# Down projections as seven products of half-size blocks, in three pieces a layer, and the attention bias kept as one row a head

## The chip, the cores and the metric

The kernel runs on one core of a Trainium2 chip, as one launch. The metric is the device time of that launch in microseconds. Below, PE is the matrix engine (its weight loads are listed apart, as PEld), DVE the vector engine, ACT the scalar engine, POOL the general-purpose engine and SP the engine that issues most DMAs. Each engine works through its own queue strictly in order; an instruction that needs another engine's result waits at the head of its queue, and all that is queued behind it waits too.

## What is computed

A trunk of two decoder layers over 512 tokens of width 1024, in float32. Layer 0 mixes tokens by a gated DeltaNet, layer 1 by sliding-window attention with a relative-position bias. Each layer ends with a gated MLP of inner width 2816, and that is where the change lies:

```python
def conv_gated_mlp(hn, w_up, conv_w, conv_b, w_down):
    u = causal_dwconv(hn @ w_up, conv_w, conv_b)
    gate, val = jnp.split(u, 2, axis=-1)
    return (jax.nn.silu(gate) * val) @ w_down

# in the trunk, for each of the two layers
h = h + conv_gated_mlp(rmsnorm(h, ffn_norm_w[layer]), ...)

# in the attention: one bias value for each head and distance between query and key
bias = rel_table[t5_bucket(dist)]
s = einsum(q, k) + bias, masked to 0 <= dist < 128
```

## The kernel before

Activations lie transposed: 128 features on the partitions, 512 tokens along the free axis. The residual `h` is eight such tiles, two neighbours of which lie in one buffer. Every float32 operand of a large product is kept as two reduced-precision parts, `hi` (a rounded copy) and `lo` (what is left), and a product is three matmuls (`mm3`, L132 to L137): hi by hi, hi by lo and lo by hi.

Weights come in stages: `load_stage` (L116) has SP load up to eight 128x256 tiles into one of two `stage` buffers. `cast` (L124) makes the two parts of one 128-wide half of a stage: ACT copies to `whi` (L128), then DVE subtracts to `wlo` (L129). There are three `whi` and three `wlo` buffers, so a cast waits until PE has finished with the cast three back.

The gated MLP (`ffn`, L830) splits the 22 tiles of the inner width into two pieces, of 12 and 10 tiles. In a piece it first makes the activations, two tiles (a pair) at a time. For a tile, `up` (L839) runs 24 matmuls of 512 columns for the gate and 24 for the value. Each result is scaled (DVE, L843), put through the width-3 convolution (ACT L846, then two DVE instructions at L848), the gate through a Silu (ACT, L863), and both are multiplied (DVE, L865). `split` then writes the two parts (ACT L140, DVE L141) into buffers handed out in turn by `wide`; there are 16 of these. When the whole piece is there, each of the eight output tiles `m` is summed over all its tiles, as 12x3 or 10x3 matmuls of 512 columns into one PSUM bank of tag `d`, and DVE adds the bank to `h[m]` (L881).

The last output tile of layer 1 goes through `final` (L891), which runs its matmuls in two halves of 256 tokens, so that the closing norm of the first half runs beside the second; two running sums feed it (DVE L898 and L904). After layer 0, `attention` normalises `h` (ACT L144, DVE L145), adds up its squares (L796) and starts with the K and V projections, whose weights are cast by the same L128 and L129.

The attention bias is made once, by `bias_rows` (L680): PE picks the table's rows by a one-hot product, DVE writes a row of 257 values a head, and POOL issues four DMAs (L691) that write that row 128 times into the scratch tensor `rb`. Later each pair of heads reads a 128x2x256 block of it (L995), and DVE adds it to the scores (L1018).

The order within each queue is set at build time by a list scheduler: it places instructions by priority (program order here) as its own estimate says that they become ready, so the order may differ from the program's, but it is fixed when the kernel runs.

## Time and profile before

| | |
|---|---|
| three timed runs | 1463.84 to 1468.73 us, median 1468.68 us |
| the profiled execution | 1466.23 us, of which the recorded span is 1464.3 us |
| TensorE clock granted, mean | 0.992 |
| PE, DVE, ACT, POOL busy share | 98%, 65%, 49%, 2% |
| down projections, one piece of 12 tiles | about 66 us (8 output tiles of 8.24 us) |

A row of the profile names the line of the code, the engine, the operation and its operands as output<-inputs; a timeline row begins with the start in us from the span's start and the duration. Matmuls overlap in the array, so the time that one adds is the distance between two starts, not its recorded duration. The release named behind an idle time is the instruction that ended the wait.

### The profile page before, as it was taken

What the parts mean: (1) busy time and instruction counts of PE and PEld (TensorE: products, weight loads), DVE (VectorE), ACT (ScalarE), POOL (GpSimd) and SP (SyncE); (2) the same over time, 40 slices, a digit from 0 to 9 for tenths busy, and PEclk for the clock granted to TensorE, in tenths of its full rate; (3) what the DMA queues carried; (4) which work ended last, traced back from release to release, by engine and by line L of the source; (5) the groups of instructions that cost most, each with busy time, mean ns of one, the idle gap of its engine ahead of it and who ended that gap; (6) DMA issues with size and microseconds to landing.
All of it is one profiled execution on the core that took longest, in us unless ns stands there. A gap on an engine that the chain in (4) does not pass through costs nothing.

```text
span 1464.3 us, 19548 instructions
## 1 busy us (share of the span) xinstructions
PE 1438.9 (98%) x7519; PEld 1167.2 (80%) x7519; DVE 951.6 (65%) x1661; ACT 718.3 (49%) x1406; POOL 22.7 (2%) x51
## 2 busy tenths in 40 slices
PE   7999999999999999999999999999999999999998
PEld 5778878878877788878888888877788888888887
DVE  5896885968835536748337765778667775356754
ACT  7764574656536424434224444678744443234432
POOL 1000000000000000000010000000000000000000
PEclk9999999999989999999999999999999999999999
DMA  5334254163346523272332223221132322322222
GB/s 153 97 93 112 84 164 122 55 195 109 109 150 219 167 91 107 70 140 93 108 116 84 89 94 126 91 73 51 46 101 86 115 79 87 121 88 87 94 72 94
DMA packets 163617, 154.79 MB, mean 106 GB/s; under 512 B 24212, under 2 KB 150725, under 8 KB 163525
## 3 DMA queue, kind: packets, MB, share of 16 engines
q1 hardware_dynamic: 160690, 151.25, 32.4%
q0 software_dynamic: 576, 2.11, 1.3%
q8 instruction: 59, 0.97, 0.3%
q10 hardware_dynamic: 2259, 0.20, 0.2%
q14 instruction: 33, 0.27, 0.1%
HBM read 134.65 MB, written 18.88 MB: 105 GB/s over the span
## 4 chain that ended last, share of the span: by engine, by line
PE 93%; DMA 4%; ACT 1%; DVE 1%; issue 0%; ACTq 0%; DVEq 0%; SPq 0%
PE d L137 26%; PE d L135 26%; PE d L136 26%; PE s L585 2%; DMA stage<-in_ffn_w_up_dram 1%; PE p L1043 1%; PE s L600 1%; PE g L1038 1%; PE s L625 1%; PE p L608 1%; PE s L562 1%; PE p L555 1%; PE g L671 1%; PE s L1013 1%; DMA ol<-od 1%; PE g L450 1%
## 5 line engine op out<-in xcount | busy, mean ns | idle before, releaser
L135 PE MATMUL d<-xh,whi 128*128 128x512 f32 x1192 | 475.7, 400 | 2.3 <-ACT whi L128 2.2
L137 PE MATMUL d<-xh,wlo 128*128 128x512 f32 x1192 | 475.3, 400 | 0.1
L136 PE MATMUL d<-xl,whi 128*128 128x512 f32 x1192 | 474.2, 398 | 0.0
L128 ACT CAST whi<-stage 128x1024 fp32r<-128x1024 f32 (+2 forms) x236 | 230.2, 977 | 340.3 <-PE d L136 312.1
L129 DVE TENSOR_TENSOR wlo<-stage,whi 128x1024 fp32r<-128x1024 f32 (+2 forms) x236 | 267.0, 1132 | 151.5 <-ACT whi L128 145.9
L135 PEld LDWEIGHTS d<-xh,whi 128*128 128x128 f32 x1192 | 225.4, 189 | 50.5 <-ACT whi L128 2.6
L136 PEld LDWEIGHTS d<-xl,whi 128*128 128x128 f32 x1192 | 225.3, 189 | 49.2 <-issue 1.2
L137 PEld LDWEIGHTS d<-xh,wlo 128*128 128x128 f32 x1192 | 225.2, 189 | 49.2 <-issue 1.4
L227 DVE SCALAR_TENSOR_TENSOR acc<-d,cwc,acc 128x511 f32<-128x511 f32 (+2 forms) x96 | 70.6, 738 | 8.8 <-ACT acc L224 8.4
L843 DVE TENSOR_TENSOR sz<-d,p6s 128x512 f32<-128x512 f32 x58 | 39.9, 687 | 55.3 <-PE d L137 53.4
L863 ACT ACTIVATE dt<-dt 128x512 f32<-128x512 f32 x44 | 27.8, 632 | 83.3 <-DVE dt L848 83.2
L137 PE MATMUL d<-sy,wlo 128*128 128x512 f32 (+1 forms) x148 | 57.4, 388 | 0.0
L135 PE MATMUL d<-sy,whi 128*128 128x512 f32 (+1 forms) x148 | 57.2, 388 | 0.0
L136 PE MATMUL d<-sy,whi 128*128 128x512 f32 (+1 forms) x148 | 57.2, 386 | 0.0
L135 PE MATMUL d<-kT,whi 128*128 128x512 f32 (+1 forms) x146 | 57.2, 394 | 0.0
L137 PE MATMUL d<-kT,wlo 128*128 128x512 f32 (+1 forms) x146 | 57.1, 391 | 0.0
L136 PE MATMUL d<-qT,whi 128*128 128x512 f32 (+1 forms) x146 | 57.0, 390 | 0.0
L848 DVE SCALAR_TENSOR_TENSOR va<-sz,fcw,va 128x511 f32<-128x511 f32 (+1 forms) x58 | 43.4, 748 | 2.7 <-ACT va L846 1.7
L848 DVE SCALAR_TENSOR_TENSOR dt<-sz,fcw,dt 128x511 f32<-128x511 f32 (+1 forms) x58 | 43.4, 748 | 1.2 <-ACT dt L846 0.2
L507 DVE TENSOR_TENSOR sT<-sT,p6s 64x31 f32<-64x31 f32 (+15 forms) x124 | 40.8, 329 | 1.9
L501 DVE TENSOR_TENSOR p6s<-sN,sT 64x31 f32<-64x31 f32 (+15 forms) x124 | 40.8, 329 | 1.8
L843 DVE TENSOR_TENSOR zl<-d,p6s 128x512 f32<-128x512 f32 x30 | 20.6, 688 | 31.2 <-PE d L137 30.9
(378 smaller groups left out, 2121.7 us busy)
## 6 DMA issues: line engine op xcount, KB each, us to landing
stage<-in_ffn_w_up_dram SPq DMA_DIRECT2D x44, 1024.0 KB, 5.1
stage<-in_a_w_in_dram SPq DMA_DIRECT2D x23, 1024.0 KB, 5.4
stage<-in_ffn_w_down_dram SPq DMA_DIRECT2D x16, 768.0 KB, 4.3
stage<-in_ffn_w_down_dram SPq DMA_DIRECT2D x16, 640.0 KB, 4.1
stage<-in_a_w_out_dram SPq DMA_DIRECT2D x8, 1024.0 KB, 4.8
zd<-sz SPq DMA_DIRECT2D x16, 256.0 KB, 2.0
od<-o SPq DMA_DIRECT2D x16, 256.0 KB, 2.9
stage<-in_b_w_q_dram SPq DMA_DIRECT2D x4, 1024.0 KB, 5.6
```

The costliest lines, as they stand in the source:

```text
L128: S.copy(hi[:, :kt, :m], src)
L129: V.tensor_tensor(lo[:, :kt, :m], src, hi[:, :kt, :m].bitcast(F32), op=ALU.subtract)
L135: PE.matmul(ps, hi[:, k, :m], xh[k], start=first and k == 0, stop=False)
L136: PE.matmul(ps, hi[:, k, :m], xl[k][:], start=False, stop=False)
L137: PE.matmul(ps, lo[:, k, :m], xh[k], start=False, stop=last and k == kt - 1)
L227: V.scalar_tensor_tensor(acc[:, d:], ps[:, : T - d], col, acc[:, d:], op0=ALU.mult, op1=ALU.add)
L501: V.tensor_tensor(tv, N[:, s, s + 1 : 32].unsqueeze(2).to_broadcast([64, n, m]), Tm[:, s : s + 1, 0:m].to_broadcast([64, n, m]), op=ALU.mult,)
L507: V.tensor_tensor(Tm[:, s + 1 : 32, 0:m], Tm[:, s + 1 : 32, 0:m], tv, op=ALU.subtract)
L585: PE.matmul(x[:, si], t[:, i, cs], S0[:, si], start=True, stop=True)
L843: V.tensor_tensor(u[:], ps[:], rs[:], op=ALU.mult)
L848: V.scalar_tensor_tensor(acc[:, d:], u[:, : T - d], tap(2 - d, t), acc[:, d:], op0=ALU.mult, op1=ALU.add)
L863: S.activation(a[:], a[:], AF.Silu)
```

## The change

**Seven products.** Two tiles of the inner width and two output tiles make a 2x2 arrangement of weight blocks (A11, A12, A21, A22, each 128x128), and the two halves of the tokens with the two inner tiles a 2x2 arrangement of activation blocks (B11 to B22, each 128x256). The four output blocks were eight block products; now they are seven, of sums and differences of the blocks (Strassen's scheme in Winograd's form). A block product is three matmuls of 256 columns. For each pair of output tiles and each piece the seven products are summed over the piece's pairs in PSUM banks of the tags d, p, s, g and d (`seven_products`).

For that, the change adds work on three engines:

- DVE, for each pair of activation tiles: four differences of 256 columns (`forms`, L917 to L920), and four `lo` parts in place of two (L930). ACT makes four `hi` copies in place of two (L929).
- POOL, for each pair of output tiles and piece: four sums or differences of weight blocks, in place in the stage (L959, L964, L965, L971), each over 128 x (pairs of the piece) x 128 values.
- ACT and DVE, for each pair of output tiles and piece: three and a half casts of the stage's halves (`cast`, and `cast_odd` for a half one, L137 and L138) in place of two whole ones. DVE adds the products to `h` in six instructions of 256 columns and two of 512, in place of two of 512 (L951).

Each pair of tiles now takes four `wide` buffers, so a piece holds four pairs at most: the 22 tiles go in three pieces, of 8, 8 and 6. The last pair of output tiles of layer 1's last piece is done as before (`plain`).

**Bias.** `rb` is now 16x384, one row a head, written by one DMA from SP; each block is read from it with a window that moves by one value a partition, and DVE reads it backwards along the keys.

```diff
+    def cast_odd(st, nk, half):
...
+        odd = slice(1, 2 * nk, 2)
+        src = st[:, odd, half * P : half * P + P]
+        S.copy(hi[:, odd, :], src)
+        V.tensor_tensor(lo[:, odd, :], src, hi[:, odd, :].bitcast(F32), op=ALU.subtract)
...
-        for u in range(4):
-            G.dma_start(
-                rb[:, 32 * u : 32 * u + 32, :], oh_t[0:16, 144:401].unsqueeze(1).to_broadcast([16, 32, 257])
-            )
...
+        SP.dma_start(rb[:], rv[0:16, 0:384])
...
-        for t0, t1 in ((0, 12), (12, 22)):
+        for t0, t1 in ((0, 8), (8, 16), (16, NF)):
...
-                    split(b[:], gp[:, j, :], lp[:, j, :])
...
+                sevens.append(forms(*f, plain))
...
+                st = load_stage(wdn, t0 * P, 2 * nk, 256 * m2)
+                if not (plain and m2 == KD // 2 - 1):
+                    seven_products(st, nk, sevens, h_pairs[m2])
+                    continue
...
+    def forms(f0, f1, plain):
+        B11, B12, B21, B22 = f0[:, HALF[0]], f0[:, HALF[1]], f1[:, HALF[0]], f1[:, HALF[1]]
+        ta, tb = r2("Ta"), r2("Tb")
+        T1, T2, T3, T4 = ta[:, HALF[0]], ta[:, HALF[1]], tb[:, HALF[0]], tb[:, HALF[1]]
+        V.tensor_tensor(T1, B12, B11, op=ALU.subtract)
+        V.tensor_tensor(T2, B22, T1, op=ALU.subtract)
+        V.tensor_tensor(T3, B22, B12, op=ALU.subtract)
+        V.tensor_tensor(T4, B21, T2, op=ALU.subtract)
...
+            S.copy(hi, src)
+            V.tensor_tensor(lo, src, hi.bitcast(F32), op=ALU.subtract)
...
+    def seven_products(st, nk, sevens, hp):
...
+        def product(ps, w, odd, form, first=True):
+            i, half = FORM[form]
+            for k in range(nk):
+                hi, lo = sevens[k][0][i][:, HALF[half]], sevens[k][1][i][:, HALF[half]]
+                wk = 2 * k + odd
+                kw = dict(skip_group_check=not first)
+                PE.matmul(ps, w[0][:, wk, :], hi, start=first and k == 0, stop=False, **kw)
+                PE.matmul(ps, w[0][:, wk, :], lo, start=False, stop=False, **kw)
+                PE.matmul(ps, w[1][:, wk, :], hi, start=False, stop=k == nk - 1, **kw)
...
+        r0, r1, r2_, r3, r4 = [bank(t)[:, 0:256] for t in ("d", "p", "s", "g", "d")]
+        w = cast(st, 2 * nk, 0)
+        G.tensor_tensor(A21, A21, A22, op=ALU.add)
+        product(r0, w, 0, "B11")
+        add(h1[:, HALF[0]], r0)
+        product(r1, w, 1, "B21")
+        add(h1[:, HALF[0]], r1)
+        G.tensor_tensor(A11, A21, A11, op=ALU.subtract)
+        G.tensor_tensor(A12, A12, A11, op=ALU.subtract)
+        w = cast(st, 2 * nk, 1)
+        product(r2_, w, 0, "T1")
+        add(h2[:, HALF[1]], r2_)
+        product(r3, w, 1, "T4")
+        add(h2[:, HALF[0]], r3)
+        G.tensor_tensor(A22, A22, A11, op=ALU.subtract)
+        w = cast(st, 2 * nk, 0)
+        product(r0, w, 0, "T2", first=False)
+        add(h1[:, HALF[1]], r0)
+        add(h2.rearrange("p (u t) -> p u t", u=2), both(r0))
+        product(r2_, w, 1, "B22", first=False)
+        add(h1[:, HALF[1]], r2_)
+        w = cast_odd(st, nk, 1)
+        product(r4, w, 1, "T3")
+        add(h2.rearrange("p (u t) -> p u t", u=2), both(r4))
...
-            SP.dma_start(b3, toep[:, 2 * p : 2 * p + 2, 0:256])
+            shifted = bass.AP(toep.tensor, toep.offset + 2 * p * 384, [[1, P], [384, 2], [1, 256]])
+            SP.dma_start(b3, shifted)
...
-                V.tensor_tensor(e3, s3, b3[:, :, 256 - W : 256], op=ALU.add)
+                V.tensor_tensor(e3, s3, b3[:, :, W - 1 :: -1], op=ALU.add)
```

The change moves the order on the queues. Three places matter below. Lines are those of each kernel's own file; after the change the helpers stand nine or more lines further down (L843 is L854, L848 is L859, L865 is L877, L145 is L154, L796 is L807), the new functions at L910 to L980.

The first place is the end of the first piece's up projections in layer 0, on DVE. Before, from the scaling of the last up result (`sz` from a bank `d`) on:

```order
L843 TENSOR_TENSOR sz_6105<-d_6080,p6s_5175 128x512
L129 TENSOR_TENSOR wlo_6165<-stage_6114,whi_6164 128x768
L848 SCALAR_TENSOR_TENSOR va_6107<-sz_6105,fcw_371,va_6107 128x511
L848 SCALAR_TENSOR_TENSOR va_6107<-sz_6105,fcw_371,va_6107 128x510
L865 TENSOR_TENSOR va_6107<-dt_6071,va_6107 128x512
L141 TENSOR_TENSOR at_5965<-va_6107,at_5964 128x512
L129 TENSOR_TENSOR wlo_6169<-stage_6116,whi_6168 128x768
L881 TENSOR_TENSOR h_4560<-h_4560,d_6126 128x512
```

And after, from the same instruction on:

```order
L854 TENSOR_TENSOR sz_5827<-d_5802,p6s_5175 128x512
L129 TENSOR_TENSOR wlo_5924<-stage_5852,whi_5923 128x1024
L859 SCALAR_TENSOR_TENSOR va_5829<-sz_5827,fcw_371,va_5829 128x511
L951 TENSOR_TENSOR h_4560<-h_4560,d_5854 128x256
L859 SCALAR_TENSOR_TENSOR va_5829<-sz_5827,fcw_371,va_5829 128x510
L877 TENSOR_TENSOR va_5829<-dt_5793,va_5829 128x512
L918 TENSOR_TENSOR o_5834<-va_5829,o_5834 128x256
L919 TENSOR_TENSOR rq_5835<-va_5829,va_5757 128x256
L920 TENSOR_TENSOR rq_5835<-va_5829,o_5834 128x256
L930 TENSOR_TENSOR vt_5842<-va_5829,ktok_5840 128x512
L930 TENSOR_TENSOR vt_5843<-o_5834,ktok_5841 128x512
L930 TENSOR_TENSOR vt_5843<-rq_5835,ktok_5841 128x512
```

Where one `lo` part followed the multiplication, three differences and three `lo` parts do, with a product's addition to `h` among them; the additions of the next products stand behind all of these.

The second place is the same moment on PE. Before, the first output tile goes through the tiles in order; its last rows, which need the last tile (`at`):

```order
L135 MATMUL d_6126<-sy_5810,whi_6122 128x512
L136 MATMUL d_6126<-sy_5811,whi_6122 128x512
L137 MATMUL d_6126<-sy_5810,wlo_6123 128x512
L135 MATMUL d_6126<-at_5964,whi_6122 128x512
L136 MATMUL d_6126<-at_5965,whi_6122 128x512
L137 MATMUL d_6126<-at_5964,wlo_6123 128x512
```

After, 44 matmuls of the first five products that do not need the last tile come first, and then these (`ktok` and `vt` hold the parts of the last pair's blocks):

```order
L946 MATMUL p_5855<-ktok_5840,whi_5859 128x256
L948 MATMUL d_5854<-sy_5498,wlo_5924 128x256
L946 MATMUL d_5854<-sy_5664,whi_5923 128x256
L947 MATMUL d_5854<-at_5666,whi_5923 128x256
L946 MATMUL s_5856<-ktok_5841,whi_5892 128x256
L948 MATMUL d_5854<-sy_5664,wlo_5924 128x256
L946 MATMUL d_5854<-ktok_5841,whi_5923 128x256
L947 MATMUL p_5855<-vt_5842,whi_5859 128x256
L948 MATMUL p_5855<-ktok_5840,wlo_5860 128x256
```

Before, 33 matmuls of 512 columns stood between the last up matmul and the first that needs the last tile; now 44 of 256 columns do.

The third place is the end of layer 0 on DVE. Before, with `wlo_7701` the first cast for the K projection, `pz` the last two tiles of `h` and `d` a finished bank:

```order
L881 TENSOR_TENSOR pz_4562<-pz_4562,d_7532 128x512
L129 TENSOR_TENSOR wlo_7701<-stage_7697,whi_7700 128x1024
L145 SCALAR_TENSOR_TENSOR xl_7653<-pz_4562,normc_101,xh_7652 128x512
L796 TENSOR_TENSOR ol_7660<-ol_7660,acc_7677 128x512
L129 TENSOR_TENSOR wlo_7740<-stage_7697,whi_7739 128x1024
L881 TENSOR_TENSOR pz_4562<-pz_4562,d_7572 128x512
```

And after, where `wlo_8455` is the first cast for the K projection:

```order
L951 TENSOR_TENSOR pz_4562<-pz_4562,d_8266 128x512
L154 SCALAR_TENSOR_TENSOR xl_8399<-pz_4561,normc_101,xh_8398 128x512
L154 SCALAR_TENSOR_TENSOR xl_8403<-pz_4561,normc_101,xh_8402 128x512
L154 SCALAR_TENSOR_TENSOR xl_8407<-pz_4562,normc_101,xh_8406 128x512
L154 SCALAR_TENSOR_TENSOR xl_8411<-pz_4562,normc_101,xh_8410 128x512
L807 TENSOR_TENSOR ol_8414<-ol_8414,acc_8416 128x512
L129 TENSOR_TENSOR wlo_8455<-stage_8451,whi_8454 128x1024
```

The first two K casts stood ahead of the last addition to `h`; now the first stands behind it, behind four splits and one sum.

More of the change, by code (lines that the diff above doesn't have):

```diff
@@ L851, in up @@
             return acc
-        for t0, t1 in ((0, 12), (12, 22)):
-            gh, gl = [], []
+        for t0, t1 in ((0, 8), (8, 16), (16, NF)):
+            plain = last and t1 == NF
+            sevens = []
             for t in range(t0, t1, 2):
@@ L859, in ffn @@
                 sv = load_stage(wup, 0, 8, DFF + t * P)
-                gp, lp = wide("G"), wide("L")
+                f = []
                 for j in range(2):
@@ L865, in ffn @@
                     V.tensor_tensor(b[:], a[:], b[:], op=ALU.mult)
[L866 to L869 removed]
+                    f.append(b)
+                sevens.append(forms(*f, plain))
+            nk = len(sevens)
             for m2 in range(KD // 2):
[L871 to L881 removed]
@@ new lines, in ffn, with last_down @@
+                w = cast(st, 2 * nk, 0)
+                ps = bank("d")
+                mm3(ps[:], w, 2 * nk, gh, gl)
+                V.tensor_tensor(h[KD - 2], h[KD - 2], ps[:], op=ALU.add)
+                w = cast(st, 2 * nk, 1)
+                def last_down(ps, ts, u):
+                    ks = range(u * nk, u * nk + nk)
+                    for k in ks:
+                        PE.matmul(ps, w[0][:, k, :], gh[k][:, ts], start=k == 0, stop=False)
+                        PE.matmul(ps, w[0][:, k, :], gl[k][:, ts], start=False, stop=False)
+                        PE.matmul(ps, w[1][:, k, :], gh[k][:, ts], start=False, stop=k == 2 * nk - 1)
```

58 lines of the change are left out of this document (35 added, 23 removed).

## Prediction

> **What bounds the kernel now.** I read the page's header, PE's waits, and then the timeline of the stages that change.
>
> ```profile
> PE 1438.9 (98%) x7519; PEld 1167.2 (80%) x7519; DVE 951.6 (65%) x1661; ACT 718.3 (49%) x1406; POOL 22.7 (2%) x51
> PE g L182 <- DMA acc<-in_ffn_conv_b_dram: 9.1, 1, 9.1
> PE g L314 <- DVE sz L282: 2.5, 1, 2.5
> PE d L135 <- ACT whi L128: 2.2, 1, 2.2
> 692.00:752.00 60.00, 60.00 (x264) 49.24 (x263) 20.85 (x25) 13.44 (x16) 0.00 (x0) 1.00 0.35 114
> 760.00:860.00 100.00, 100.00 (x439) 82.04 (x438) 71.53 (x91) 43.84 (x55) 1.77 (x4) 1.00 0.29 96
> ```
>
> PE is busy 98%. Its longest wait, 9.1 us, lies at the start, and no wait in the list stands in a down stage. The two window rows (length, then PE, PEld, DVE, ACT, POOL, clock) show a down stage, where DVE works 20.85 of 60 us, and an up stage, where it works 71.53 of 100; PE fills both at full clock. So fewer PE cycles in a down stage come off the total, as long as DVE, with 65% of spare time there, can take what the change gives it.
>
> **The change: what PE saves.** The stream's pace is the distance between starts.
>
> ```profile
> 683.73 0.39 PE L135 MATMUL d<-xh,whi 128*128 128x512 f32 x1
> ...
> 688.99 0.39 PE L137 MATMUL d<-xh,wlo 128*128 128x512 f32 x1
> 1447.41 0.28 PE L136 MATMUL d<-nt,whi 128*128 128x256 f32 x1
> ...
> 1452.47 0.28 PE L137 MATMUL d<-kT,wlo 128*128 128x256 f32 x1
> ```
>
> The first two rows bound one up product of 24 matmuls: 5.26/23 = 0.2287 us each. The other two stand 43 matmuls apart in the last output tile: 5.06/43 = 0.1177 us at 256 columns, hardly more than half, with a weight load each. Before, layer 0 has 22x8x3 = 528 wide matmuls, 120.8 us; layer 1 has 498 and 60 narrow ones, 121.0 us. After, layer 0 has 11 pairs x 4 x 21 = 924 narrow ones, 108.8 us; layer 1 has 861 and 36 narrow and 18 wide ones, 109.7 us. **PE saves 23.3 us.**
>
> **The turn from up to down, pieces of 8 (four times).** Before:
>
> ```profile
> 689.42 0.69 DVE L843 TENSOR_TENSOR sz<-d,p6s 128x512 f32<-128x512 f32 x1
> 690.07 0.82 ACT L128 CAST whi<-stage 128x768 fp32r<-128x768 f32 x1
> 690.79 0.81 ACT L846 ACTIVATE va<-sz,normc,fcw 128x512 f32<-128x512 f32 x1
> 691.79 1.53 DVE L848 SCALAR_TENSOR_TENSOR va<-sz,fcw,va 128x511 f32<-128x511 f32 x2
> 693.36 0.69 DVE L865 TENSOR_TENSOR va<-dt,va 128x512 f32<-128x512 f32 x1
> 694.09 0.62 ACT L140 CAST at<-va 128x512 fp32r<-128x512 f32 x1 [2.48 <-DVE va L865]
> 694.74 0.69 DVE L141 TENSOR_TENSOR at<-va,at 128x512 fp32r<-128x512 f32 x1 [0.69 <-ACT at L140]
> ```
>
> The last up product ends at 689.22 (688.99 + 0.23); its `lo` part is there 6.2 us later, and PE meanwhile has 33 x 0.2287 = 7.5 us of work. It never waits. After the change the cover is 48 x 0.1177 = 5.65 us, and DVE has more to do, by these rows:
>
> ```profile
> L129 DVE TENSOR_TENSOR wlo<-stage,whi 128x1024 fp32r<-128x1024 f32 x172 | 210.0, 1222 | 93.6 <-ACT whi L128 88.3 <-PE d L135 1.6 <-PE d L137 0.3
> L129 DVE TENSOR_TENSOR wlo<-stage,whi 128x768 fp32r<-128x768 f32 x32 | 30.6, 958 | 39.8 <-ACT whi L128 39.7
> L881 DVE TENSOR_TENSOR h<-h,d 128x512 f32<-128x512 f32 x16 | 11.0, 689 | 33.4 <-PE d L137 33.4
> 1451.02 0.42 DVE L941 TENSOR_TENSOR pz<-pz,d 128x256 f32<-128x256 f32 x1 [3.14 <-PE d L137]
> 1451.99 0.43 DVE L924 TENSOR_TENSOR ol<-ol,acc 128x256 f32<-128x256 f32 x1 [0.15 <-ACT acc L922]
> 921.04 1.23 DVE L129 TENSOR_TENSOR wlo<-stage,whi 128x1024 fp32r<-128x1024 f32 x1 [0.21 <-ACT whi L128]
> 922.18 0.75 DVE L145 SCALAR_TENSOR_TENSOR xl<-pz,normc,xh 128x512 fp32r<-128x512 f32 x1
> 922.85 0.69 DVE L796 TENSOR_TENSOR ol<-ol,acc 128x512 f32<-128x512 f32 x1
> L128 ACT CAST whi<-stage 128x1024 fp32r<-128x1024 f32 x172 | 180.2, 1050 | 200.0 <-PE d L136 171.8 <-DMA stage<-in_ffn_w_up_dram 13.7 <-DMA stage<-in_a_w_in_dram 7.5
> ```
>
> The last three DVE rows show that an independent instruction starts some 0.08 us before the one ahead has ended; I take 0.07 off at such places. Times from the end of the last up product: scaling 0.2 to 0.9; the third weight cast (its `whi` buffer is only now free) on ACT to 1.25, on DVE to 2.5; two convolution steps with a product's addition (0.42) between them to 4.25; multiplication 4.95; three differences 6.2; three `lo` parts 6.85, 7.5, 8.1; the additions of the second and third product 8.45 and 8.85. The sixth product adds into the third's bank, so it starts at 8.95, where PE without any wait would be at 62 x 0.1177 = 7.3. DVE, late by now, goes through three more additions, the half cast, and the next weight pair's first cast, done at 12.45. POOL then makes two blocks from that pair's stage; behind them stands the cast that the pair's fifth product needs.
>
> The trace has no POOL instruction with two inputs. Its nearest rows are
>
> ```profile
> L300 POOL TENSOR_SCALAR_AFFINE_SELECT acc<-acc 128x128 f32<-128x128 f32 x1 | 0.6, 609 | 0.1
> masks.py:199 POOL TENSOR_SCALAR_AFFINE_SELECT ident<-ident 128x128 f32<-128x128 f32 x1 | 0.3, 283 | 0.0
> ```
>
> Four times the elements make 1.13 to 2.44 us for a block sum over four pairs, three times 0.85 to 1.83 over three. With 1.13 that fifth product starts at 17.3 where 132 x 0.1177 = 15.5 would do: 1.8 us lost. With 2.44 it is 4.1. I take the middle, 1.8 us an instruction: 2.8 lost. After that DVE needs 8.3 us (3 x 1.22 + 0.69 for casts, 6 x 0.42 + 2 x 0.69 for additions) in 84 x 0.1177 = 9.9, and keeps up. **Four turns: 11.2 us** (7.2 to 16.4).
>
> The Trainium skill, "GPSIMD Engine Reference", section on performance versus the Vector engine, gives 4,497 ns for a two-input add of 2,048 float32 values a partition; an estimate from it is 1.12 us for 512 and 0.84 for 384, the lower ends of my bounds, and with them the whole sum below would be 1.7 us under the time before. No run here shows it yet.
>
> **Layer 0's piece of 6.** A weight pair is now 63 x 0.1177 = 7.4 us of PE, and DVE needs 3 x 0.958 + 0.56 + 3.9 = 7.3, with nothing left to catch up a late turn. From the last up product to the first K cast, 66 DVE instructions stand in line: 10 casts of 0.958, 4 half ones of 0.56 (an estimate from the casts' slope), one of 1.22, 24 additions of 0.42 and 8 of 0.69, 8 splits of 0.75, and 7.0 for the scaling, two convolution steps, the multiplication, three differences, three `lo` parts and a sum. That is 41.5 us; less 50 overlaps of 0.07, plus 0.4 for the start and ACT's cast and 0.9 of waiting for POOL, 39.7. PE has 4 x 7.4 + 6 K matmuls that need no `lo`, 31.0. So **8.7 us are lost, 9.6 with POOL at its middle** (to 11.6). Before, as the order shows, these casts stood ahead of the last addition, and PE did not wait.
>
> **Layer 1's piece of 6 and the end.** The same three weight pairs, then closing norm work: 35.3 us of DVE up to the addition that frees the first half's norm (the L941 row), against 3 x 7.4 + 18 x 0.2287 + 1.7 of transposes + 18 x 0.1177 = 30.3 for PE: 5.0 lost. Behind it DVE, not PE, sets the end, so 0.7 of the saving counted there is not seen. **5.7 lost, 6.6 with POOL at its middle** (to 8.6).
>
> **The rest at nothing.** In the up stages DVE goes from 16.4 to 19.2 us in each 22 (four differences of 0.43 and the `lo` parts of two more tiles, one of them half); casts stand two products ahead, 11 us, and cover it; without cover each turn would lose more, which is counted above. Weight DMAs carry the same bytes, and a stage's last cast comes 8 to 11 us before the first cast of the stage that takes its buffer, against 4.3 us to land:
>
> ```profile
> stage<-in_ffn_w_down_dram SPq DMA_DIRECT2D x16, 768.0 KB, 4.3
> L1018 DVE TENSOR_TENSOR dt<-s,sz 128x512 f32<-128x512 f32 x18 | 12.3, 683 | 1.4 <-PE g L1038 1.1 <-ACT dt L1031 0.3
> ```
>
> The bias row's DMA is queued on SP after the loads of the up pair and before the first down stage, whose buffer is not yet free, so nobody waits for it. Reading it backwards I put at the 683 ns of the L1018 row, which never waited for a DMA; twice as long would be 32 x 0.35 = 11 us of DVE, hidden beside PE in attention or not. That it could gain is excluded: PE waits for none of it now.
>
> **Sum:** -23.3 + 11.2 + 9.6 + 6.6 = **+4.1 us** (-1.7 to +13.3 by POOL alone). On the profiled execution, 1466.23 us (span 1464.3 and 1.9 around it), that is 1470.3; it ran 2.4 below the median of the three runs, 1468.7, and on the median it is 1472.8. I forecast **1472 us**, no change that can be told: about 0.5% (7.3 us) is what a measurement of this kernel can tell from none.
>
> **Rivals.** *DVE and POOL hold each other up* (slower). Each POOL sum reads two operands from SBUF, and so does each `lo` cast that starts or waits beside it. The trace of before has no such meeting, so nothing speaks for or against the price. If every second of the 28 POOL instructions in the pieces of 6 holds DVE's queue for its 0.85 us, and one in each of the four turns for 1.13, 16.4 us come on top of the sum with POOL's lower ends: -1.7 + 16.4 = +14.7, **1483 us**. It decides only where DVE is already late; in the steady pairs of 8 it has 1.6 us to spare. The Trainium skill, "SBUF — State Buffer", section "Who interferes with whom", states just this: a vector instruction with two SBUF inputs and a GpSimd instruction that reads SBUF share a port, and whoever comes second waits for the whole of the other.
>
> *DVE catches up* (faster). If what DVE is late by is not its queue but only the data's own chain, the turns lose 0.5 us each (scaling to `lo` parts 6.4 us beside 5.65 of cover, POOL quick), the end of layer 0 4.1 (an addition, four splits, a sum and a cast behind the last product, less the six K matmuls), layer 1's end 0.7: -23.3 + 6.8 = -16.5. Half way between that and the sum with quick POOL is -9, **1460 us**. For it speaks that DVE has 65% to spare in the down stage today; against it, that the queue is in order and the additions stand behind the forms.
>
> *POOL is slow*: the upper ends, +13.3, **1482 us**.
>
> **How the numbers follow.** The forecast 0.45 (0.36 of it within 0.5%, 0.09 above), the port 0.22, slow POOL 0.08, DVE catching up 0.25 (0.22 of it faster by over 0.5%, 0.03 within). So faster 0.22, same 0.39, slower 0.39. The range, 1459 to 1487, reaches from just below the half-way faster case to just above the port's price; about a tenth is left out on each side (no lateness of DVE at all, or more meetings with POOL).
>
> **What would show it.** Right: 256-column products at 0.118 us; PE idle before the last pair's matmuls of each first weight pair (L946 to L948, released by DVE L930 or L951), about 2 to 3 us a turn; PE waiting some 9 us for the first K cast; DVE over 90% busy in the pieces of 6; POOL's L964 at 0.8 to 1.8 us. The port: casts of 128x1024 longer than 1.22 us when POOL works. Wrong: no idle time on PE at the turns, a pace other than 0.118, or waits on DMA in a down stage.

## The result, and the profile after

The changed kernel took 1489.9 us (median of four runs, 1486.8 to 1491.8) against 1466.4 us before (four runs, 1463.8 to 1468.7): a ratio of 1.015, with a 95% interval of 1.012 to 1.018. It is slower, by 23.6 us. The forecast was no change, 1472 us, and the range ended at 1487, so both are wrong. The profiled execution took 1486.8 us, with a span of 1485.0, 20.7 above that of before. Executions of one and the same kernel differ by several us with the clock that was granted to PE (before ran from 1460.3 us at a mean clock of 0.997 to 1476.8 at 0.988), so a stage length from one profile is read together with the clock in it.

The page's header and the waits of PE that are new or grew most, of those in the down stages and behind them (engine, line, what it waited for: us in total, times, longest):

```profile
PE 1431.5 (96%) x8272; PEld 1193.6 (80%) x8272; DVE 1127.0 (76%) x1977; ACT 764.2 (51%) x1480; POOL 165.8 (11%) x139
PE d L946 <- DVE h L951: 7.2, 5, 2.0
PE p L946 <- ACT sy L929: 5.3, 4, 1.8
PE d L948 <- DVE wlo L129: 3.9, 7, 0.7
PE d L144 <- ACT whi L128: 3.3, 1, 3.3
PE s L946 <- DVE pz L951: 2.4, 5, 1.0
PE s L946 <- DVE h L951: 2.3, 4, 0.6
```

PE is busy 96% where it was 98%. Most of its new waits stand in the seven products (L946 to L948), behind DVE or behind an ACT copy that itself waits for DVE.

The table sets stages side by side, each from the start of its first matmul to that of the next stage; the last row ends where the four small matmuls of the closing norm start. Two columns belong to the experiments below: the bias part alone, and the best kernel found.

| us | before | bias alone | after | after without sums | plain ends, sums on DVE |
|---|---|---|---|---|---|
| all up to the first up stage | 550.4 | 546.6 | 546.7 | 549.3 | 548.5 |
| layer 0, up stages | 248.7 | 244.3 | 244.3 | 244.3 | 244.3 |
| layer 0, down stages | 120.9 | 120.9 | 132.4 | 115.3 | 113.0 |
| K products to the end of attention | 168.0 | 168.2 | 174.8 | 175.1 | 168.8 |
| layer 1, up stages | 243.6 | 243.6 | 243.6 | 243.6 | 243.6 |
| layer 1, down stages to the closing norm | 125.8 | 125.8 | 136.4 | 120.5 | 118.6 |

Against before, after loses 11.5, 6.8 and 10.6 us in the down stages and at the start of attention, and gains 4.4 us in layer 0's up stages and 3.7 ahead of them: +20.8, the 20.7 us of the two spans but for rounding. The loss is larger than the forecast had it, and there is a gain that the forecast had excluded. The 3.7 us ahead of the up stages are a matter of the clock alone: that stretch less its half-clock losses is 541.9 us before, 543.3 after and 541.5 with the bias alone.

**A turn, close up.** At the second turn of layer 0, the last up matmul starts at 771.09. Four stretches of the windows view (length, then PE, PEld, DVE, ACT, POOL, clock) show PE running out of work, waiting, and then running at about half clock:

```profile
771.30:775.80 4.50, 4.50 (x40) 4.48 (x38) 3.37 (x5) 1.82 (x3) 1.73 (x1) 1.00 0.00 0
775.80:780.00 4.20, 1.21 (x9) 0.82 (x7) 4.13 (x8) 1.24 (x3) 0.00 (x0) 1.00 0.00 0
780.00:783.70 3.70, 3.70 (x19) 3.70 (x20) 2.94 (x6) 1.71 (x4) 0.00 (x0) 0.54 0.00 0
783.70:787.00 3.30, 3.26 (x27) 3.06 (x27) 3.27 (x6) 1.99 (x2) 0.00 (x0) 1.00 0.09 16
```

In the second stretch DVE works 4.13 of 4.20 us: it is the late one. Its timeline shows why. The rows below are DVE's in the last pair of the up stage, and behind the "..." the scaling of the last up result; the second fence holds POOL's rows of the same moment:

```profile
763.87 2.45 DVE L859 SCALAR_TENSOR_TENSOR va<-sz,fcw,va 128x511 f32<-128x511 f32 x2
766.36 1.67 DVE L877 TENSOR_TENSOR va<-dt,va 128x512 f32<-128x512 f32 x1
768.06 1.40 DVE L917 TENSOR_TENSOR o<-va 128x256 f32<-128x256 f32 x1
...
773.81 0.68 DVE L854 TENSOR_TENSOR zl<-d,p6s 128x512 f32<-128x512 f32 x1
```

```profile
764.10 1.68 POOL L964 TENSOR_TENSOR stage<-stage 128x512 f32<-128x512 f32 x1 [5.60 <-DVE wlo L129]
765.85 1.62 POOL L965 TENSOR_TENSOR stage<-stage 128x512 f32<-128x512 f32 x1
767.44 1.74 POOL L959 TENSOR_TENSOR stage<-stage 128x512 f32<-128x512 f32 x1
```

The multiplication (L877) takes 1.67 us in place of 0.69 and the first difference 1.40 in place of 0.42. Each ends some 0.3 to 0.6 us after a POOL sum has ended, that is, nearly one length of its own later, as if it had been held until then. POOL's sums take 1.62 to 1.74 us here, while the shortest of 64 such sums took 1.28, so POOL is held too. That the sums are the cause is for the experiments to show. The scaling starts at 773.81, 2.5 us after the last up product has ended; the prediction had 0.2. At the other three turns of 8 it starts 1.8, 2.4 and 2.5 us late. Summed over DVE, what its instructions take beyond the usual time of their shape (the median without sums, differences over 0.1 us) is 35 us, 22 of it in the last pairs of the six up stages.

### The profile page after: what moved, and what is told of

Read it like the earlier page. It is cut to its first block, busy times and chain, and to the rows that moved or that the text cites. A ratio compares the mean times of both kernels' runs of the same rounds, so it can differ in the third digit from the quotient of the medians.

```text
span 1485.0 us, 21679 instructions
## 1 busy us (share of the span) xinstructions
PE 1431.5 (96%) x8272; PEld 1193.6 (80%) x8272; DVE 1127.0 (76%) x1977; ACT 764.2 (51%) x1480; POOL 165.8 (11%) x139
## 5 line engine op out<-in xcount | busy, mean ns | idle before, releaser
L145 PE MATMUL d<-xl,whi 128*128 128x512 f32 x1192 | 473.2, 398 | 0.0
L129 DVE TENSOR_TENSOR wlo<-stage,whi 128x1024 fp32r<-128x1024 f32 (+1 forms) x243 | 297.6, 1226 | 111.2 <-ACT whi L128 110.4
L128 ACT CAST whi<-stage 128x1024 fp32r<-128x1024 f32 (+1 forms) x243 | 248.9, 1028 | 256.5 <-PE d L145 127.0
L145 PEld LDWEIGHTS d<-xl,whi 128*128 128x128 f32 x1192 | 225.1, 189 | 47.4 <-issue 1.0
L959 POOL TENSOR_TENSOR stage<-stage 128x512 f32<-128x512 f32 (+1 forms) x23 | 38.3, 1666 | 714.5 <-DMA stage<-in_ffn_w_down_dram 527.9
L854 DVE TENSOR_TENSOR sz<-d,p6s 128x512 f32<-128x512 f32 x58 | 39.9, 688 | 33.6 <-PE d L146 31.0
L859 DVE SCALAR_TENSOR_TENSOR va<-sz,fcw,va 128x511 f32<-128x511 f32 (+1 forms) x58 | 47.4, 817 | 2.1 <-ACT va L857 1.2
L859 DVE SCALAR_TENSOR_TENSOR dt<-sz,fcw,dt 128x511 f32<-128x511 f32 (+1 forms) x58 | 47.5, 819 | 1.0
L964 POOL TENSOR_TENSOR stage<-stage 128x512 f32<-128x512 f32 (+1 forms) x23 | 31.3, 1363 | 143.8 <-DVE wlo L129 143.8
L929 ACT CAST sy<-va 128x512 fp32r<-128x512 f32 (+1 forms) x22 | 11.5, 524 | 66.9 <-DVE va L877 66.9
L965 POOL TENSOR_TENSOR stage<-stage 128x512 f32<-128x512 f32 (+1 forms) x23 | 42.6, 1850 | 1.6
L516 DVE TENSOR_TENSOR sT<-sT,p6s 64x31 f32<-64x31 f32 (+15 forms) x124 | 40.9, 330 | 2.0
L877 DVE TENSOR_TENSOR va<-dt,va 128x512 f32<-128x512 f32 x44 | 35.8, 813 | 1.5
L948 PE MATMUL d<-sy,wlo 128*128 128x256 f32 x129 | 36.8, 285 | 0.0
```

The lines of the kernel that those rows point to most:

```text
L128: S.copy(hi[:, :kt, :m], src)
L129: V.tensor_tensor(lo[:, :kt, :m], src, hi[:, :kt, :m].bitcast(F32), op=ALU.subtract)
L145: PE.matmul(ps, hi[:, k, :m], xl[k][:], start=False, stop=False)
L516: V.tensor_tensor(Tm[:, s + 1 : 32, 0:m], Tm[:, s + 1 : 32, 0:m], tv, op=ALU.subtract)
L859: V.scalar_tensor_tensor(acc[:, d:], u[:, : T - d], tap(2 - d, t), acc[:, d:], op0=ALU.mult, op1=ALU.add)
L877: V.tensor_tensor(b[:], a[:], b[:], op=ALU.mult)
```

## The experiments

Three theories stood against each other when the runs began. Theory A: POOL's sums hold DVE, and PE's longer waits halve its clock on top. R1: the sums cost only as links in the chain from stage to cast. R2: DVE's own queue is too long, with or without POOL.

**Without the sums.**

```diff
-        G.tensor_tensor(A21, A21, A22, op=ALU.add)
...
-        G.tensor_tensor(A11, A21, A11, op=ALU.subtract)
-        G.tensor_tensor(A12, A12, A11, op=ALU.subtract)
...
-        G.tensor_tensor(A22, A22, A11, op=ALU.subtract)
```

> The four block sums of POOL for each pair of output tiles are left out (the casts read the unsummed blocks, so the outputs of the down projections are not the reference's). Theory A, two parts: (1) POOL's sums of the first weight pair run in the last pair of the up stage, and each holds a DVE instruction with two SBUF inputs until it has ended (1.67 us in place of 0.75 and 0.69), so DVE reaches the last scaling of a piece some 2.2 us late; (2) PE's wait at the turn is then long enough for the granted clock to fall to one half for 3 to 7 us afterwards. By A the turns of 8 lose some 2.5 us in place of 7.5, the steady weight pairs nothing, the L0 piece of 6 with the attention start 8 less: 20 to 30 us less than after, 1460 to 1470, and few half-clock stretches in the down stages. Rival R1: the sums cost only as links in the chain from stage to cast, as the prediction had it: 6 to 9 us less, about 1482. Rival R2: DVE's own queue is all of it: within 3 us of after, 1487 to 1492.

Measured: 1452.6 us, a ratio to before of 0.989 (0.987 to 0.992), 37 us less than after and below what even theory A gave. DVE's rows at the same turn (the last up product ends at 768.43) and the longest of PE's waits in the down stages:

```profile
760.65 0.75 DVE L859 SCALAR_TENSOR_TENSOR va<-sz,fcw,va 128x510 f32<-128x510 f32 x1
761.44 0.69 DVE L877 TENSOR_TENSOR va<-dt,va 128x512 f32<-128x512 f32 x1
762.16 0.42 DVE L917 TENSOR_TENSOR o<-va 128x256 f32<-128x256 f32 x1
...
768.63 0.69 DVE L854 TENSOR_TENSOR zl<-d,p6s 128x512 f32<-128x512 f32 x1 [1.96 <-PE d L146]
```

```profile
PE p L946 <- ACT sy L929: 2.1, 3, 1.0
```

DVE now waits 1.96 us for PE, where PE had waited for DVE; the scaling starts at 0.2 at every turn. A piece of 8 takes 39.5 to 40.7 us in place of 46.2 to 47.5. R2 falls at the turns: 92 instructions on a mostly idle engine are the difference. The start of attention keeps its 7 us, so that part is not POOL's.

**The same sums, into a scratch row.** The casts no longer depend on them:

```diff
-        G.tensor_tensor(A21, A21, A22, op=ALU.add)
+        junk = row("gr")[:].rearrange("p (k c) -> p k c", k=4)[:, 0:nk, :]
+        G.tensor_tensor(junk, A21, A22, op=ALU.add)
```

(and so for the other three).

> POOL does the same four sums over the same blocks, but writes them to a scratch row that nobody reads; the casts read the unsummed blocks (outputs not the reference's). So POOL's length is out of the chain, and its meeting with DVE stays. Theory A: most of the loss stays, 1480 to 1488, with DVE instructions of 1.4 to 1.7 us beside POOL's. Rival R1 (length in the chain): as the kernel without sums. If the two are alike, the port is not the cause.

Measured: 1489.9 us, a ratio of 1.016 (1.012 to 1.019): exactly after's time. DVE and POOL at its second turn, and PE's wait that grew:

```profile
768.63 3.48 DVE L859 SCALAR_TENSOR_TENSOR dt<-zl,fcw,dt 128x511 f32<-128x511 f32 x2
772.03 0.68 DVE L854 TENSOR_TENSOR sz<-d,p6s 128x512 f32<-128x512 f32 x1
```

```profile
769.93 1.62 POOL L966 TENSOR_TENSOR gr<-stage 128x512 f32<-128x512 f32 x1
771.63 1.63 POOL L972 TENSOR_TENSOR gr<-stage 128x512 f32<-128x512 f32 x1
```

```profile
PE d L946 <- DVE h L951: 16.6, 6, 3.4
```

Two convolution steps take 3.48 us in place of 1.53. The scaling, 0.68 us, reads one operand from PSUM and is not held. Nobody waits for these sums, yet they cost all that the real ones cost. From the first up stage on, the queues of PE, DVE and ACT hold the same operations in the same order as in the kernel without sums (4944, 1211 and 740), so it isn't a new order either. R1 is out, and the meeting with DVE is shown.

**PE kept busy.**

```diff
+        def idle(n):
+            for _ in range(n):
+                PE.matmul(spare, w0[0][:, 1, :], sevens[0][0][0][:, HALF[0]], start=True, stop=True)
...
+        if turn_:
+            idle(25)
         product(r0, w, 0, "B11")
...
+        if k_next:
+            idle(28)
```

> PE gets 25 more matmuls of 256 columns (2.9 us), whose results nobody reads, ahead of the first product of each down stage, and 28 (3.3 us) behind the last product of layer 0, ahead of the first K products. All else as after. They fill time in which PE waits anyway. Theory A part 2 (the clock falls because PE waited): no half-clock stretch behind the turns of layer 0's second and third piece, layer 1's first and second, and the attention start, which in the profile of after cost 1.6, 1.6, 3.4, 1.6 and 3.2 us: some 10 us less than after, about 1480. If the clock falls for other reasons: nothing gained, 1489 to 1492, and half-clock stretches at the same places.

Measured: 1491.2 us, a ratio of 1.016 (1.013 to 1.019), no gain. What the half clock loses in the down stages and at the start of attention (a window's length times one less its clock, summed) fell from 11.7 us to 5.1, and the time did not follow. The order of PE's queue came out anew, so three turns kept waits of 2.8 to 3.1 us in all, with a half-clock stretch behind them. At the start of attention the two kernels compare well; the first fence is after's, the second this one's:

```profile
924.40:927.80 3.40, 0.15 (x1) 0.00 (x0) 3.40 (x6) 1.77 (x3) 0.78 (x2) 0.86 0.46 160
927.80:933.70 5.90, 5.86 (x14) 4.35 (x15) 5.71 (x7) 2.46 (x5) 0.00 (x0) 0.50 0.30 102
```

```profile
931.70:936.00 4.30, 1.78 (x10) 1.24 (x10) 4.30 (x7) 1.88 (x3) 0.00 (x0) 1.00 0.18 62
936.00:942.00 6.00, 6.00 (x28) 4.91 (x27) 4.97 (x7) 3.32 (x6) 0.00 (x0) 1.00 0.53 175
```

The stretch at 0.50 is gone, PE starts 28 matmuls in it where it started 14, and the stage is 3.5 us shorter, 0.8 of it a shorter wait. So a wait of 3.3 us there does cost nearly as much again in clock. At the turns DVE is still the one that PE waits for, and the added matmuls take 2.9 us themselves: the pieces of 8 came out 0.3 us shorter to 1.4 us longer than after's. So the second part of theory A is seen at the start of attention only. As a 10 us term it is not shown, and what the half clock costs at the turns this experiment cannot separate from what was added.

**The first pair of each piece as eight products.**

```diff
+                if m2 == 0:
+                    for j in range(2):
+                        w = cast(st, 2 * nk, j)
+                        ps = bank("d")
+                        mm3(ps[:], w, 2 * nk, gh, gl)
+                        V.tensor_tensor(h[2 * m2 + j], h[2 * m2 + j], ps[:], op=ALU.add)
+                    continue
```

> The first pair of output tiles of each piece is done as eight products (two outputs of 24 or 18 wide matmuls), the other three as seven (layer 1's last pair plain as it was). PE has 1.1 us more to do at each piece (5.2 to 6.3 in all); behind the last up product it has 18 wide matmuls of 512 columns that don't need the last pair (4.1 us, against 5.2 us of seven-product matmuls) and then those that need f1 and f0 alone; POOL's sums move off the end of the up stage. Theory A: waits, collisions and half-clock stretches at the turns go, 5 to 6 us each: 15 to 25 us less than after, 1465 to 1475. Rival R2 (DVE's queue alone, turns at 2.8 as predicted): at most 5 us less, 1485.

Measured: 1473.4 us, a ratio of 1.004 (1.001 to 1.007), in the range of theory A. Three seven-product pairs of 8 then take 29.9 us (252 matmuls at 0.1185): the steady pairs do keep up. What is left stands in the first pair, 14.2 to 17.0 us for 48 x 0.2287 = 11.0, still waiting for the last tile's parts.

**The sums in quarters.**

```diff
+            for k in range(nk):
+                G.tensor_tensor(dst[:, k, :], x[:, k, :], y[:, k, :], op=op)
```

> Each POOL sum over four pairs is issued as four of 128x128 (three over three pairs), with the same results. Theory A in its strict form (whichever of a DVE instruction with two SBUF inputs and a POOL sum comes second waits until the other has ended): a meeting costs DVE at most the length of a short POOL instruction, some 0.3 to 0.6 us by the 128x128 rows, in place of up to 1.1 us; the lengthening summed over DVE falls from 36 us to 20 or less, if POOL's queue leaves a gap between two that DVE takes; time 1470 to 1482. If the two share the port element by element instead, the summed lengthening stays at some 36 us and the time at 1487 to 1492.

Measured: 1483.7 us, a ratio of 1.011 (1.008 to 1.014), between the two expectations. POOL's group (line, operation, shape, count | busy us, mean ns):

```profile
L961 POOL TENSOR_TENSOR stage<-stage 128x128 f32<-128x128 f32 x340 | 212.7, 662 | 808.8 <-DMA stage<-in_ffn_w_down_dram 525.8 <-DVE sz L854 134.9 <-DVE wlo L129 100.2
```

DVE's multiplication and first difference at the second turn:

```profile
773.76 0.83 DVE L877 TENSOR_TENSOR va<-dt,va 128x512 f32<-128x512 f32 x1
774.63 0.57 DVE L917 TENSOR_TENSOR o<-va 128x256 f32<-128x256 f32 x1
```

They are 0.15 us over their usual time each, where after had 0.98, and the lengthening over DVE fell from 35 us to 12, as it should where each waits for the whole of the other. The scaling starts at 0.2 at every turn. But a short sum takes 0.66 us on average, the time in which it is held included, so the four sums of a weight pair take 16 x 0.66 = 10.6 us in place of 6.8, more than PE's 9.9 us for the pair, and ACT's casts wait 65 us for POOL in place of 51. The pieces of 8 take 46.5 to 46.8 us in this profile, hardly less than after's: DVE was relieved, and the chain from stage to cast took its place. The gain of 6 us in the medians is not found in any stage of the profile.

**The sums on DVE.**

```diff
-        G.tensor_tensor(A21, A21, A22, op=ALU.add)
+        V.tensor_tensor(A21, A21, A22, op=ALU.add)
```

(and so for the other three).

> The four block sums go from POOL to DVE (0.69 us each over 512 elements, 0.56 over 384), same results, no POOL work in the down stages. Theory A: no DVE instruction longer than its usual time; but DVE has 60 us more to do, 8.3 + 2.8 = 11.1 us in a steady weight pair of 8 against PE's 9.9, and 9.5 against 7.4 in the pairs of 6: pairs 2 to 4 lose 1.2 us (12 of them, 14 us), those of 6 some 2.1 (7 of them, 15 us), while the turns lose some 3 us less than after. In all about as slow as after, 1480 to 1500: the port costs about as much as if DVE did the sums itself. If the lengthening was not what cost the time, the same sums on DVE make it slower than after by 25 us or more, above 1510.

Measured: 1464.9 us, a ratio of 0.998 (0.996 to 1.000), 25 us less than after and well below the expectation. That DVE with 60 us of extra work is 25 us better than DVE beside POOL is the plainest sign of what the meetings cost. The expectation was wrong on the steady pairs: a piece of 8 takes 41.6 to 41.7 us, so its three steady pairs lose at most 0.7 us each and not 1.2. I had added 11.1 us of DVE from recorded durations; with the overlap of some 0.08 us at each of about 16 instructions it is 9.8, just PE's 9.9.

**Before, with scratch sums.**

```diff
+                for u in range(2):
+                    for x, y in ((0, 1), (1, 0)):
+                        junk = row("gr")[:].rearrange("p (k c) -> p k c", k=4)
+                        G.tensor_tensor(junk, sts[u][:, x : x + 4, 0:P], sts[u][:, y : y + 4, P : 2 * P], op=ALU.add)
```

> The kernel before, with four POOL sums of 128x512 for each pair of output tiles and piece (64 in all), read from the down stages and written to a scratch row that nobody reads. Theory A: DVE instructions with two SBUF inputs are lengthened by up to 1.1 us beside them here too, but DVE works only a third of a down stage and 72% of an up stage, with PE's cover of 7.5 us at a turn, so the time stays: 1464 to 1472. If the port costs time by itself (by holding PE, ACT or the DMAs), 1475 or more.

Measured: 1469.0 us, a ratio of 1.001 (0.998 to 1.003), as expected. PE, DVE and ACT have the order of before throughout, DVE's instructions are lengthened by 33 us in all, nearly as in after, and it costs nothing that can be told: where DVE has time, being held is free.

**Plain ends.** Beside the first pair, the last pair of layer 0 is plain; both tiles' parts come before the differences; and the first pair leaves the last two tiles to the end:

```diff
+                if m2 == 0 or (l == 0 and t1 == NF and m2 == KD // 2 - 1):
...
+                    for ks in (range(2 * nk - 2), range(2 * nk - 2, 2 * nk)) if m2 == 0 else (range(2 * nk),):
+                        for j in range(2):
+                            for k in ks:
```

> As the kernel with the first pair of each piece plain, and three steps more: the last pair of layer 0 is plain too; the parts of both activation tiles come before the four differences; and in the first pair both output tiles are summed over all tiles but the last two before either takes those (36 wide matmuls, 8.2 us, of cover for the last tile's parts; 24 or 27 in the pieces of 6). Theory A: against the kernel before, PE saves 23.3 - 6.8 (four first pairs of 8 at 1.1, three plain pairs of 6 at 0.8) = 16.5 us; the turns lose under 1.5 us each, POOL's meetings fall where DVE has time; the K start and its half clock (6.9 us in after) go. 1453 to 1461. Rival R2 (the queue of DVE as such): no better than the kernel with the first pair plain, 1468 to 1475.

Measured: 1448.7 us, a ratio of 0.987 (0.984 to 0.990), below theory A's 1453 to 1461, which held no gain from the bias; R2's 1468 to 1475 is far off. Pieces of 8 run at nearly PE's pace (40.9 to 41.4 us), and the time from the K products to the end of attention is back at 168.9 us.

**The pieces alone, the bias alone, and both.** Three kernels with eight products throughout. The first has only

```diff
-        for t0, t1 in ((0, 12), (12, 22)):
+        for t0, t1 in ((0, 8), (8, 16), (16, NF)):
```

> The kernel before, eight products throughout, but in pieces of 8, 8 and 6 tiles. PE has the same matmuls. Behind the last up product stand 21 wide matmuls (4.8 us) of the first output tile in place of 33 (7.5 us), 15 (3.4 us) in the piece of 6, against the 6.2 us that the last tile's parts take, unless the second output tile fills in. If smaller pieces are part of what the change lost: 1.4 us a turn of 8 and 2.8 a piece of 6, some 10 us, about 1476. If the loss comes with the seven products alone (POOL's sums, differences, more casts and additions): within 4 us of before, 1463 to 1471.

the second only the bias part of the change,

```diff
-    rb = dp.tile([16, P, 257], F32, name="rb")
+    rb = dp.tile([16, 384], F32, name="rb")
...
-        for u in range(4):
-            G.dma_start(
...
+        SP.dma_start(rb[:], rv[0:16, 0:384])
...
-                V.tensor_tensor(e3, s3, b3[:, :, 256 - W : 256], op=ALU.add)
+                V.tensor_tensor(e3, s3, b3[:, :, W - 1 :: -1], op=ALU.add)
```

> The kernel before with the bias part of the change alone (one row a head, one DMA from SP, read backwards on DVE). The prediction put it at nothing: 1463 to 1471, the additions of 128x512 at 0.68 us as before. If reading backwards were slower on DVE or the shifted window slower to load, 1475 or more, in the attention stage.

the third both.

> The kernel before with eight products throughout, in pieces of 8, 8 and 6, and the bias part of the change as well. In the kernel with pieces alone nearly all of the loss stood in the first piece of layer 0, where the down weights came late behind POOL's four bias DMAs. If so, the pieces cost nothing once the bias is one row a head: 1453 to 1460, as the kernel with the bias alone, and every down stage at its pace (44.0 and 33.2 us). If small pieces cost time by themselves: 1464 to 1468.

Measured: 1477.0 (1.007, 1.004 to 1.010), 1455.6 (0.992, 0.990 to 0.995) and 1460.5 us (0.996, 0.993 to 0.999). By the medians the bias alone gains 11.5 us (by the ratio's interval 7 to 15), by the two profiles 8.3. Two things are seen in its trace. Before, POOL's four DMAs write the 2.1 MB of `rb` from 620 us on (a source's rows: engine, the issues' durations in ns, first and last start; then the time to landing; then ACT's cast that waited):

```profile
L691 POOL DMA_DIRECT2D rb<-gr x4: 630/630/757, 619.8 to 621.8; - x4
DMA to landing us min/median/max: 8.2/16.3/23.9
```

```profile
647.71 1.04 ACT L128 CAST whi<-stage 128x1024 fp32r<-128x1024 f32 x1 [9.39 <-DMA stage<-in_ffn_w_up_dram]
```

The same stretch of the up stage before, and then with the bias alone:

```profile
619.00:648.80 29.80, 27.60 (x120) 22.29 (x120) 13.15 (x19) 7.68 (x11) 2.62 (x4) 1.00 0.84 141
648.80:652.50 3.70, 3.56 (x8) 2.38 (x9) 3.23 (x4) 1.62 (x3) 0.00 (x0) 0.54 0.02 4
```

```profile
619.00:648.80 29.80, 29.80 (x132) 24.46 (x131) 20.48 (x26) 13.52 (x17) 0.00 (x0) 1.00 0.38 128
648.80:652.50 3.70, 3.70 (x18) 3.04 (x17) 3.46 (x5) 0.99 (x2) 0.00 (x0) 1.00 0.10 31
```

The DMA engines were busy 0.84 of the time, the up weights came late, PE waited 2.2 us and ran at half clock afterwards: 4.4 us, which the single DMA of 24 KB saves. The other part, 3.8 us in the profiles, lies ahead of the up stages, with a half-clock stretch at 420 us in layer 0's mixer. Before:

```profile
417.40:420.40 3.00, 3.00 (x69) 2.48 (x69) 0.60 (x1) 0.73 (x2) 0.00 (x0) 0.97 0.83 286
420.40:433.60 13.20, 13.20 (x75) 10.44 (x73) 3.82 (x6) 1.62 (x2) 0.30 (x1) 0.50 0.20 63
```

Behind 3 us in which 65 of 69 matmuls were 32x32, PE ran at half clock for 13 us, though it never waited; that loses 6.6 us. The build-time order changes with the bias part from some 350 us on. The dip at 420 to 440 us is in all three profiled kernels with the old bias and in none of the eleven with the new one, but it does not come with the order alone: in the kernel with scratch sums, which has before's order, it is a quarter as long, and one execution of before had a mean clock of 0.997, which leaves 4.4 us of loss for the whole kernel. So the 4.4 us of the DMAs are shown; that the bias part causes the share at 420 us is not.

The pieces' 10 us came as expected, but for another reason: 10.2 of them stand in the first piece of layer 0 (54.2 us), where the down weights now stood behind the same four DMAs (one of ACT's casts waited 11.9 us for them), and the other pieces run at their pace. With the new bias the first piece takes 44.0 us too. Against the bias alone, the pieces then cost 3.4 us by the two spans and 4.9 by the medians, which is not explained.

**Plain ends, sums on DVE.** The kernel with plain ends, with

```diff
-        G.tensor_tensor(A21, A21, A22, op=ALU.add)
+        V.tensor_tensor(A21, A21, A22, op=ALU.add)
```

and so for the other three.

> The kernel with plain ends (first pair of each piece and the last of layer 0 as eight products, both tiles' parts first, two banks), with the block sums on DVE in place of POOL. Theory A: once DVE has time, POOL's meetings cost nothing, so taking them away gains nothing: within 3 us of the kernel with plain ends, 1446 to 1452. If the port still cost time there, 1443 or less; if DVE is short again in the pairs done as seven products, 1455 or more.

Measured: 1443.5 us, a ratio of 0.984 (0.982 to 0.987), the fastest of all. It is 5.2 us below plain ends with POOL's sums, and not within 3: nearly the 1443 at which the meetings still cost time there. Layer 0's three pieces, as windows:

```profile
639.03:679.69 40.66, 40.66 (x301) 38.69 (x300) 36.19 (x59) 14.73 (x17) 0.00 (x0) 1.00 0.26 86
767.59:808.25 40.66, 40.66 (x301) 38.69 (x300) 36.18 (x59) 14.74 (x17) 1.22 (x3) 1.00 0.27 87
874.17:905.81 31.64, 31.64 (x200) 28.27 (x198) 30.90 (x55) 18.42 (x27) 3.94 (x8) 1.00 0.34 109
```

PE is never idle in them. With POOL's sums the third took 34.96 us (32.63 of PE): in a piece of 6 DVE works 30.9 of 31.6 us, so there the meetings still cost.

## Why the prediction was wrong, step by step

| term | predicted | measured |
|---|---|---|
| PE's saving, 0.1177 us a matmul of 256 columns | -23.3 | the pace held: 0.1177 where PE does not wait |
| four turns of pieces of 8 | +11.2 (7.2 to 16.4) | +29.6 (6.6, 7.6, 7.5, 7.9) |
| layer 0's piece of 6 to the K products | +9.6 (8.7 to 11.6) | +16.0 (9.4 in the piece, 6.6 behind it) |
| layer 1's piece of 6 and the end | +6.6 (5.7 to 8.6) | +6.3 |
| bias | 0, a gain excluded | -8.1 (4.4 in the up stages, 3.7 ahead of them) |

The measured column is that of the two profiles, and adds up to +20.5 of the 20.7 us between their spans.

**The step that failed first: "the rest at nothing", in the up stages.** It had DVE at 19.2 of 22 us in a pair of the up stage and called that covered. POOL's sums of the first weight pair run in just that pair, and DVE's instructions there were lengthened by 3.8 to 4.0 us at the turns of 8: DVE was busy 20.3 to 20.7 of the last 22 us, without the sums 18.1 to 18.3. The chain at the turn was then started at 1.8 to 2.5 us and not at 0.2, and the term of the four turns became 29.6 in place of 11.2. Without sums each piece of 8 loses 0 to 1.2 us, so DVE's own queue, which the forecast priced at 1.8 us a turn even with the quickest POOL, was not the cause; on this point the rival in which DVE catches up, with 0.5 a turn, was nearer.

**The rival was right in kind and too cheap.** "DVE and POOL hold each other up" counted one meeting a turn and 14 in the pieces of 6, 16.4 us, and gave the steady pairs of 8 time to spare; the profile shows five lengthened DVE instructions at each turn of 8, four of them before the last up product has ended. It came out at 1483; without the 8.1 us of the last row, which no case held, this kernel would have been near 1498 (an estimate). The Trainium skill, "SBUF — State Buffer", section "Who interferes with whom", says that the shared port is an exclusive lock; the trace agrees, with 1.67 us in place of 0.69 and the fall from 35 to 12 us with short sums. The estimate from the Trainium skill, "GPSIMD Engine Reference", section "Performance versus the Vector engine" (1.12 and 0.84 us), was near: the shortest sums took 1.28 and 1.00. So POOL's own length, on which the bounds rested, mattered least.

**The bias: a row was quoted and not followed.** The third row of the prediction's first fence, PE's 2.2 us for `whi`, was the mark of the four DMAs. I wrote that the list held no wait in a down stage, and of the bias that "PE waits for none of it now"; it waited, in an up stage, for weights that stood behind it. And I looked for order changes only where the code had changed, not from 350 us on; whether those have to do with the half clock at 420 us stays open.

**The K start.** The 9 us wait for the first K cast did not come as one: 9.4 us went in the piece itself, and behind it came one wait of 3.3 us and 5.9 us at half clock. DVE's share in that piece was 33.5 of 39.1 us, 86% and not over 90%. Without sums 4.2 us in the piece and 7 at the start of attention stay, 11.2 of the 16.0, and with the last pair plain the start of attention loses nothing, while the first pair alone as eight products did not help it (175.7 us). So here the prediction's reason, DVE's queue, was right. Its sum was a little off: the terms as listed make 41.6 us and then 39.4, not 39.7, which is 8.4 lost and not 8.7.

**What held.** No wait on a DMA in a down stage; L964 at 1.39 us on average; PE idle at each first weight pair behind L951 and L929, by 1.9 to 3.0 us. That the measured time lies only 3 us above the range is partly luck: the 8.1 us that the forecast had excluded cover part of the loss that it had missed.

## What to carry to other kernels

A helper on an idle engine is not free because it is idle: ask whose port it uses, and look at the stretch in which it will run, which is where its input lands and not where the code names it. Cost it there by what the busy engine has left. When a change has two parts, price each against every wait of the profile, the short ones in other stages too; here the small part gained 4.4 us at a wait that a row of before's profile had shown, and together with 3.7 us of clock that hid more than a quarter of what the large part lost. Once the sums were on DVE and the pieces' ends plain, both together gained 23.6.

## What the runs showed of the hardware

- A POOL sum of two SBUF operands and a DVE instruction of two SBUF operands hold each other up: DVE's were lengthened by up to 1.1 us, POOL's sums took up to 2.53 us in place of 1.28. Of 77 DVE instructions with one operand in PSUM that ran beside a POOL sum in after, none was lengthened (0.67 to 0.69 us for 128x512, 0.41 to 0.42 for 128x256).
- The granted clock fell to one half, for 3.4 or 6.8 us at a time, about single waits of PE of 1.8 to 3.3 us in after's down stages and behind them, but not at every such wait: of two of 1.79 us there one was followed by it and one was not, nor was one of 2.39 us (before with scratch sums, at 477 us) or of 2.52 us (PE kept busy, at 933 us). It also fell with PE never idle: for 13 us behind the 32x32 matmuls, whose part in it is not shown, and at 238 and 333 us in four of fourteen profiles.
- A sum of a quarter of the size took a third of the time (0.445 us against 1.28 at the shortest).
- Reading the bias block backwards costs DVE nothing: 0.685 us for 128x512 in place of 0.683.
